# A hybrid decoder layer in float32 pairs: the order of cast, dependent work and low part in each step, both heads' scores in one step, banks emptied a step later, the norm two cycles later, and another order of the first output block

## The chip, the cores and the metric

The kernel runs on one core of a Trainium2 chip. The metric is the device time of one execution in microseconds (us), taken as the median of the runs. TensorE (PE in the profile; PEld is its weight load) multiplies matrices into eight PSUM banks. VectorE (DVE), ScalarE (ACT) and GpSimd (POOL) do the elementwise work, SyncE (SP) issues most of the transfers. Each engine works through its own instructions in order; semaphores hold an instruction back until what it reads or overwrites is ready.

## The reference

One layer of 16 stick-breaking attention heads beside 16 groups of a short gated convolution, for 256 tokens and 16 meta tokens, with 4096 channels:

```
h = rmsnorm(x, norm_g)
q, k, v, g_attn, b_conv, c_conv, h_conv, z_conv = split(h @ w_in)      # 4096 x 16384
z    = q . k / sqrt(128)                                # per head, strictly causal
a    = exp(log_sigmoid(z) + sum over later keys of log_sigmoid(-z))
o    = group_rmsnorm((a @ v) * silu(g_attn))
y    = group_rmsnorm(b_conv * conv3(c_conv * h_conv) * silu(z_conv))
out  = rmsnorm(x + concat(o, y) @ w_out)                # meta tokens dropped
```

## The kernel before

**Float32 from pairs.** Every weight tile arrives as `raw` (128 x 1024 float32). ACT casts it to `wh` (the high part, L399), DVE takes the rest `wl = raw - wh` (the **low part**, L395), and each product is three matmuls: low activations by `wh`, high activations by `wh`, high activations by `wl` (L424 to L426 for 258 columns, L432 to L435 for 512). `wh` and `wl` have rings of six buffers, so a tile is split five pieces ahead of its use.

**Pieces.** The program is a list of pieces, and the main loop (L970) goes through them one **step** a piece. The input projection has 8 groups of two heads. A piece `p` is a quarter of a projection block (k, v, c or h of one head, 24 matmuls). `A` and `B` are the two halves of a column pair of q, g, b, z for both heads (12 matmuls each). For the pairs listed in `SJ` (and `OUT_SJ` in the output projection) seven products do the work of eight: such a pair has four pieces A, B, T, U with 6, 3, 6 and 6 matmuls, T and U being sums of A and B that DVE forms (L409 to L414). I call such a pair a **seven**, the other a **plain** pair. Each group first has a **row zone** (R) of four plain pairs, with the last two blocks of the group before it between them (the order p p A B, four times), and then a **sum zone** (S) of twelve cycles A B T U p p. The output projection takes column blocks 8 to 11 of 16 pairs each, and eight narrow pieces at the end. A piece `m` reloads and casts a mixed activation tile that an earlier group has written to DRAM, and holds no matmul.

**What a step issues, before:** the matmuls of piece i; the split of piece i+5 (cast, and low part or the sums right behind it); the emptying of PSUM banks of what ended with piece i (`plain_block`, `open_rows`, `evict`, `out_sums`, `out_block`); then the tasks that are due (`run_tasks`). From the end of group 0 up to the eighth piece from the end the engines' order is the order in which the program issues (`manual_schedule`, L982).

**Tasks of a group** (`plan_group`, L828), counted in steps from `f`, the last step of the group's sum zone: the gates' SiLU and the transposition of q at f+1; for the two heads `scores` at f+4 and f+6, `weights` at f+7 and f+9, `trans` at f+10 and f+13, `po` at f+13 and f+17. `scores` is two matmuls `z`, one step later the mask on DVE (`zm`, L744, L746) and Abs, Tanh and Ln on ACT (L749 to L751). `weights` is one subtraction, two running sums and another subtraction on DVE (L757 to L761), one step later four Exp on ACT (`za`, L768 to L771). `trans` is a transposition on DVE (`ya`, L777) and, over the next two steps, copies of 32 x 96 squares into the one buffer `at`, half on ACT (L565), half on DVE (L563). `po` multiplies `at` by v (L788 to L792). The v blocks go through a like transposition (`vt`, `yv`, `vv`; L577 to L591).

**In the sum zone of the next group** the earlier group's convolution is transposed (`ct`), its squares are summed, `norm` (11 small DVE instructions, L692 to L694) gives the factors, and `mix` transposes the result on PE into a bank (`mxh` for the attention half, `mxc` for the convolution half, L707). In this zone there is one bank for all of it, the one in which the p blocks are summed, so `mix` has to wait until the last p block there has been emptied (L572, L578, L597 or L602 on DVE).

Of the kernel before, what the change touches and what calls it, by code (L numbers as in the profile page):

```python
# [8 lines left out]
F32 = mybir.dt.float32  # L9
# [6 lines left out]
P = 128  # L16
# [30 lines left out]
OUT_FIRST = (0, 1, 2, 3, 4, 5, 6, 7, 8, 9, 10, 14, 11, 12, 13, 15)  # L47
OUT_SJ = (8, 9, 10, 11, 12, 13)

# [6 lines left out]
def sevens(g):  # L56

    return OUT_SJ if g >= GROUPS else SJ if g else ()

# [5 lines left out]
def in_pieces():  # L65
# [45 lines left out]
def kernel(ctx, tc, xt, xin, xm, par, fg, w1, w2, out):  # L111
# [7 lines left out]
    wk.tile([P, 16], F32, name="pad_wk")  # L119
# [30 lines left out]
    ms = [("m", g) for g in range(GROUPS - 1)]  # L150
# [207 lines left out]
    def split(i):  # L358
# [9 lines left out]
        if p[0] == "m":  # L368
# [3 lines left out]
            nc.vector.tensor_tensor(out=lo, in0=t, in1=h.bitcast(F32), op=ALU.subtract)  # L372
# [8 lines left out]
            return  # L381
# [15 lines left out]
        for q in range(parts):  # L397
            c = slice(q * w // parts, (q + 1) * w // parts)
            nc.scalar.copy(out=h[:, c], in_=t[:, c])  # L399
            if not two or p[0] == "A":  # L400
                low(c)
        if two and p[0] == "A":
            sums[p] = t
        elif two:

            a = sums.pop(("A",) + p[1:])
            s = wp.tile([P, 1024], F32, tag="tt", name=f"t{i}", bufs=1)
# [7 lines left out]
            sums[("T",) + p[1:]], sums[("U",) + p[1:]] = s, t  # L415
# [199 lines left out]
    def plain_block(u, b, e):  # L615
# [3 lines left out]
        elif b == 1:  # L619
            v_block(u, ps[:, :L], after(e, 6 if u % 2 == 0 else 3))  # L620
# [114 lines left out]
    def scores(g, u):  # L735
        q = gr[g]["h"][0]
        kt = hd[2 * g + u, "k"]
        z = bank(f"z{g}_{u}")
        T.matmul(out=z[:, :144], lhsT=q[:, 0, u], rhs=kt[:, :144], start=True, stop=True)
        T.matmul(out=z[:, 144:ZW], lhsT=q[:, 1, u], rhs=kt, start=True, stop=True)  # L740
        yield 1
        zm = wk.tile([P, 512], F32, tag="u2", name=f"zm{g}_{u}", bufs=2) if u else wk.tile([P, 448], F32, tag="zm", name=f"zm{g}_{u}")
        zm = zm[:, :ZW]
        V.scalar_tensor_tensor(out=zm[:, :144], in0=z[:, :144], scalar=rq[:, 0:1], in1=zmask[:, P:],  # L744
                               op0=ALU.mult, op1=ALU.add)
        V.scalar_tensor_tensor(out=zm[:, 144:], in0=z[:, 144:ZW], scalar=rq[:, 1:2], in1=zmask,  # L746
# [365 lines left out]
```

## Time and profile before

| what | value |
|---|---|
| median of 3 runs | 1938.75 us (1937.78 to 1939.67) |
| the profiled execution | 1940.01 us, of which the span of the trace is 1938.1 us |
| PE, DVE, ACT, POOL busy | 95%, 81%, 59%, 7% of the span |
| mean granted clock of TensorE | 0.972 |
| from group to group (start of step f+1) | 195.5 us first, then 194.6 to 195.1 us |
| transfers | 393.64 MB, 203 GB/s in the mean |

The span is the time from the first to the last instruction; the rest of the execution lies around it. A busy PE is not a PE at its peak, since matmuls overlap. So the table is read as "PE is the engine on which nearly everything waits", and the question is where it stands idle or at a low clock.

### The profile page before, as it was taken

Reading aid. Unit: us, or ns where it says so; the run is one execution under the profiler, and the core shown is the slowest. Engines: PE = TensorE matmul, PEld = TensorE weight load, DVE = VectorE, ACT = ScalarE, POOL = GpSimd, SP = SyncE. Lnnn points to the kernel's source line nnn. Section 1 sums busy time; section 2 is a strip of 40 time slices with the busy share of each in tenths; the row PEclk is TensorE's granted clock in tenths of the full one; section 3 lists DMA queues with packets and bytes.
Section 4 is the critical chain, followed back from the end, with each engine's and each line's share of the span. In section 5 each row is a group of like instructions: output and inputs, shape, how many; then the busy total and the mean of one; then the engine's idle time right before and its main releaser. Section 6 shows DMA issues by size and latency. Waiting matters only on the chain.

```text
span 1938.1 us, 29646 instructions
## 1 busy us (share of the span) xinstructions
PE 1844.5 (95%) x10998; PEld 1653.0 (85%) x10998; DVE 1563.0 (81%) x2114; ACT 1147.1 (59%) x1756; POOL 136.6 (7%) x192
## 2 busy tenths in 40 slices
PE   9999899989998999899989998999899989999997
PEld 7899798979897989798979897989798967788897
DVE  6766788778877887788778887888788878998986
ACT  6645655655566556656565656565656575555554
POOL 2021010001000100010001000100010122000000
PEclk9999899989998999999999999999999989999999
DMA  8965456645664566456635663566366655575665
GB/s 306 317 222 191 153 200 222 207 151 197 218 217 143 199 222 220 142 196 220 226 140 197 218 227 136 201 211 235 134 205 207 229 173 182 193 246 205 230 204 185
DMA packets 116064, 393.64 MB, mean 203 GB/s; under 512 B 13008, under 2 KB 18256, under 8 KB 115920
## 3 DMA queue, kind: packets, MB, share of 16 engines
q1 hardware_dynamic: 111888, 388.08, 58.4%
q10 hardware_dynamic: 4032, 3.67, 0.5%
q8 instruction: 86, 1.41, 0.3%
q14 instruction: 58, 0.48, 0.1%
HBM read 380.17 MB, written 11.53 MB: 202 GB/s over the span
## 4 chain that ended last, share of the span: by engine, by line
PE 81%; DVE 8%; ACT 7%; issue 3%; DMA 1%; POOL 0%; DVEq 0%; ACTq 0%; SPq 0%; POOLq 0%
PE P L432 14%; PE P L434 14%; PE P L435 14%; PE mm L424 11%; PE mm L425 11%; PE mm L426 11%; DVE wl L395 3%; ACT wh L399 2%; DVE zl L759 1%; DVE at L563 1%; ACT L751 1%; ACT zl L751 1%; ACT L768 1%; ACT L750 1%; PE po L792 0%
## 5 line engine op out<-in xcount | busy, mean ns | idle before, releaser
L395 DVE TENSOR_TENSOR wl<-raw,wh 128x1024 fp32r<-128x1024 f32 (+3 forms) x756 | 852.3, 1145 | 267.9 <-ACT wh L399 256.6
L399 ACT CAST wh<-raw 128x1024 fp32r<-128x1024 f32 (+3 forms) x756 | 715.2, 974 | 396.3 <-PE mm L425 169.8
L424 PE MATMUL mm<-xs,wh 128*128 128x258 f32 (+1 forms) x2048 | 592.2, 289 | 0.0
L426 PE MATMUL mm<-xs,wl 128*128 128x258 f32 (+1 forms) x2048 | 588.7, 287 | 0.0
L425 PE MATMUL mm<-xs,wh 128*128 128x258 f32 (+1 forms) x2048 | 588.6, 287 | 0.0
L424 PEld LDWEIGHTS mm<-xs,wh 128*128 128x128 f32 x2048 | 390.8, 191 | 6.2 <-issue 1.6
L425 PEld LDWEIGHTS mm<-xs,wh 128*128 128x128 f32 x2048 | 390.7, 191 | 4.7
L426 PEld LDWEIGHTS mm<-xs,wl 128*128 128x128 f32 x2048 | 390.2, 191 | 0.0
L432 PE MATMUL P<-wh,xs 128*128 128x512 f32 x604 | 241.8, 400 | 2.1 <-ACT wh L399 2.1
L434 PE MATMUL P<-wh,xs 128*128 128x512 f32 x604 | 239.8, 397 | 0.0
L435 PE MATMUL P<-wl,xs 128*128 128x512 f32 x604 | 239.3, 396 | 0.0
L399 ACT CAST wh<-t 128x1024 fp32r<-128x1024 f32 (+1 forms) x108 | 112.3, 1040 | 169.4 <-DVE t L409 145.6
L432 PE MATMUL P<-wh,mixl 128*128 128x512 f32 (+1 forms) x392 | 149.9, 382 | 4.4 <-ACT wh L399 4.1
L435 PE MATMUL P<-wl,mixh 128*128 128x512 f32 (+1 forms) x392 | 149.6, 382 | 1.3 <-DVE wl L395 1.2
L434 PE MATMUL P<-wh,mixh 128*128 128x512 f32 (+1 forms) x392 | 148.9, 380 | 0.0
L435 PEld LDWEIGHTS P<-wl,xs 128*128 128x128 f32 x604 | 114.0, 189 | 27.6
L432 PEld LDWEIGHTS P<-wh,xs 128*128 128x128 f32 x604 | 114.4, 189 | 26.0 <-ACT wh L399 2.3
L434 PEld LDWEIGHTS P<-wh,xs 128*128 128x128 f32 x604 | 114.1, 189 | 22.5
L409 DVE TENSOR_TENSOR t<-raw,raw 128x1024 f32<-128x1024 f32 (+1 forms) x108 | 132.2, 1224 | 0.4
L395 DVE TENSOR_TENSOR wl<-t,wh 128x1024 fp32r<-128x1024 f32 (+1 forms) x108 | 131.9, 1221 | 0.0
L432 PEld LDWEIGHTS P<-wh,mixl 128*128 128x128 f32 x392 | 74.7, 190 | 17.5 <-ACT wh L399 4.5
L435 PEld LDWEIGHTS P<-wl,mixh 128*128 128x128 f32 x392 | 74.4, 190 | 15.5 <-DVE wl L395 3.5
(249 smaller groups left out, 2084.7 us busy)
## 6 DMA issues: line engine op xcount, KB each, us to landing
raw<-w SPq DMA_DIRECT2D x614, 512.0 KB, 4.2
lent<-sumd SPq DMA_DIRECT2D x49, 512.0 KB, 5.9
raw<-w SPq DMA_DIRECT2D x32, 384.0 KB, 4.0
raw<-xin SPq DMA_DIRECT2D x8, 512.0 KB, 5.0
xr<-xt SPq DMA_DIRECT2D x15, 272.0 KB, 5.4
sumd<-lent SPq DMA_DIRECT2D x7, 512.0 KB, 2.9
raw<-mixd SPq DMA_DIRECT2D x7, 512.0 KB, 4.3
res<-xin SPq DMA_DIRECT2D x12, 256.0 KB, 4.6
```

Of the source, the lines that this page charges most:

```text
L395: nc.vector.tensor_tensor(out=lo[:, c], in0=t[:, c], in1=h[:, c].bitcast(F32), op=ALU.subtract)
L399: nc.scalar.copy(out=h[:, c], in_=t[:, c])
L409: nc.vector.tensor_tensor(out=s[:, :2 * hw].rearrange("p (a b) -> p a b", a=2), in0=a[:, :2 * hw].rearrange("p (a b) -> p a b", a=2), in1= ...
L424: nc.tensor.matmul(out=o, lhsT=h, rhs=x[:, 0, s:], start=k == 0, stop=False)
L425: nc.tensor.matmul(out=o, lhsT=h, rhs=x[:, 1, s:], start=False, stop=False)
L426: nc.tensor.matmul(out=o, lhsT=lo, rhs=x[:, 0, s:], start=False, stop=k == KC - 1)
L432: nc.tensor.matmul(out=o, lhsT=a[1], rhs=h, start=key not in begun, stop=False)
L434: nc.tensor.matmul(out=o, lhsT=a[0], rhs=h, start=False, stop=False)
L435: nc.tensor.matmul(out=o, lhsT=a[0], rhs=lo, start=False, stop=last)
L563: V.tensor_copy(out=o, in_=x)
L750: A.activation(out=l, in_=l, func=AF.Tanh, scale=0.5)
L751: A.activation(out=l, in_=l, func=AF.Ln, scale=0.5, bias=half)
```

## The change

Six things are changed; the arithmetic of each is as it was, but for two pairs of the first output block.

1. Within a step the program now issues the cast, then the tasks, then the low part or the sums (`split` returns a closure, `lows` runs it at the step's end). Up to the end of group 0's first zone the low part still follows its cast.
2. `plain_block`, `open_rows`, `evict`, `out_sums` and `out_block` become tasks of the next step.
3. `scores` takes both heads: four matmuls at f+3, both masks, Abs and Tanh at f+4, both Ln at f+5.
4. `weights` moves to f+6 and f+8, `trans` to f+8 and f+10, `po` to f+11 and f+14. The SiLU of the second half goes to f+2, the transposition of v to the step in which its block is emptied.
5. In the sum zone `squares` goes from slot 4 to 5, `norm` from behind slot 4 to slot 6, `mix` from slots 6 and 8 to 8 and 10 (slot c is piece B of the cycle c, counted from 0).
6. The first output block takes its pairs in another order, pairs 12 and 13 are plain there, and the pieces `m` stand at other places.

```diff
-OUT_FIRST = (0, 1, 2, 3, 4, 5, 6, 7, 8, 9, 10, 14, 11, 12, 13, 15)
+OUT_FIRST = (0, 1, 2, 3, 4, 5, 6, 8, 7, 9, 14, 10, 15, 11, 12, 13)
+MIXED = {(1, "A"): 2, (3, "A"): 3, (5, "A"): 4, (6, "B"): 5, (9, "A"): 6}
-    return OUT_SJ if g >= GROUPS else SJ if g else ()
+    return OUT_SJ[:4] if g == GROUPS else OUT_SJ if g > GROUPS else SJ if g else ()
...
-            v_block(u, ps[:, :L], after(e, 6 if u % 2 == 0 else 3))
+            v_block(u, ps[:, :L], after(e, 1))
...
-    def scores(g, u):
+    def scores(g):
         q = gr[g]["h"][0]
+        z, zm, l = {}, {}, {}
+        for u in range(2):
+            kt = hd[2 * g + u, "k"]
+            z[u] = bank(f"z{g}_{u}")
+            T.matmul(out=z[u][:, :144], lhsT=q[:, 0, u], rhs=kt[:, :144], start=True, stop=True)
+            T.matmul(out=z[u][:, 144:ZW], lhsT=q[:, 1, u], rhs=kt, start=True, stop=True)
         yield 1
...
+            A.activation(out=l[u], in_=zm[u], func=AF.Abs)
+        for u in range(2):
+            A.activation(out=l[u], in_=l[u], func=AF.Tanh, scale=0.5)
+        yield 1
+        for u in range(2):
+            A.activation(out=l[u], in_=l[u], func=AF.Ln, scale=0.5, bias=half)
+            gr[g]["z", u] = zm[u], l[u]
...
         later(after(f, 1), silu, g, "h")
-        later(after(f, 1), silu, g, "c")
         later(after(f, 1), q_t, g)
-        for u, at_ in enumerate(((4, 7, 10, 13), (6, 9, 13, 17))):
-            for k, fn in zip(at_, (scores, weights, trans, po)):
+        later(after(f, 2), silu, g, "c")
+        later(after(f, 3), scores, g)
+        for u, at_ in enumerate(((6, 8, 11), (8, 10, 14))):
+            for k, fn in zip(at_, (weights, trans, po)):
                 later(after(f, k), fn, g, u)
...
+        later(slot(g + 1, 5), squares, g, "c")
+        later(slot(g + 1, 6), norm, g)
+        later(slot(g + 1, 8), mix, g, "h")
+        later(slot(g + 1, 10), mix, g, "c")
...
+        while halved < until:
+            lows()
+            r = split(halved)
+            halved += 1
+            if r:
+                rest.append(r)
+        if i <= top[0]:
+            lows()
...
-                plain_block(*p[1], i)
+                later(i + 1, plain_block, *p[1], i)
...
-                evict(p[1])
+                later(i + 1, evict, p[1])
...
         run_tasks(i)
+        lows()
```

**ACT in the row zone**, heads of group 4: what stands from the second head's Abs to the first head's Exp. `zl4_0` and `zl4_1` are the two heads' logarithms, `za` their weights, `wh428` the cast of piece 428. Before:

```order
L399 CAST wh428_9821<-raw428_9692 128x1024
L749 ACTIVATE zl4_1_9833<-zm4_1_9830 128x416
L750 ACT_TABLE_LOAD
L750 ACTIVATE zl4_1_9833<-zl4_1_9833 128x416
L751 ACT_TABLE_LOAD
L751 ACTIVATE zl4_1_9833<-zl4_1_9833,half_120 128x416
L399 CAST wh429_9851<-raw429_9722 128x1024
L768 ACT_TABLE_LOAD
L768 ACTIVATE za4_0_9855<-zs4_0_9825 128x256
```

Now, from the first head's Abs on:

```order
L762 ACTIVATE zl4_0_9738<-zm4_0_9737 128x416
L762 ACTIVATE zl4_1_9743<-zm4_1_9742 128x416
L764 ACTIVATE zl4_0_9738<-zl4_0_9738 128x416
L764 ACTIVATE zl4_1_9743<-zl4_1_9743 128x416
L401 CAST wh426_9776<-raw426_9634 128x1024
L767 ACT_TABLE_LOAD
L767 ACTIVATE zl4_0_9738<-zl4_0_9738,half_120 128x416
L767 ACTIVATE zl4_1_9743<-zl4_1_9743,half_120 128x416
L401 CAST wh427_9808<-raw427_9679 128x1024
L401 CAST wh428_9831<-raw428_9720 128x1024
L784 ACT_TABLE_LOAD
L784 ACTIVATE za4_0_9836<-zs4_0_9811 128x256
```

The first head's Exp no longer stands behind the second head's Abs, Tanh and Ln, and two table loads are gone: a group now has three of them, where it had five.

**DVE at the same place.** `zs` and the scans into `zl` are the weights, `wl429` is the low part of piece 429. Before:

```order
L757 SCALAR_TENSOR_TENSOR zs4_0_9825<-zm4_0_9752,zl4_0_9755 128x416
L759 SCALAR_TENSOR_TENSOR zl4_0_9755<-one_118,zs4_0_9825 128x144
L759 SCALAR_TENSOR_TENSOR zl4_0_9755<-one_118,zs4_0_9825 128x272
L761 TENSOR_TENSOR zs4_0_9825<-zm4_0_9752,zl4_0_9755 128x416
L744 SCALAR_TENSOR_TENSOR zm4_1_9830<-z4_1_9804,rq_124,zmask_113 128x144
L746 SCALAR_TENSOR_TENSOR zm4_1_9830<-z4_1_9804,rq_124,zmask_113 128x272
L395 TENSOR_TENSOR wl429_9852<-raw429_9722,wh429_9851 128x1024
L395 TENSOR_TENSOR wl430_9891<-raw430_9772,wh430_9890 128x1024
L757 SCALAR_TENSOR_TENSOR zs4_1_9894<-zm4_1_9830,zl4_1_9833 128x416
```

Now:

```order
L777 TENSOR_TENSOR zs4_0_9811<-zm4_0_9737,zl4_0_9738 128x416
L397 TENSOR_TENSOR wl427_9809<-raw427_9679,wh427_9808 128x1024
L607 TENSOR_TENSOR cc9_9834<-mm9_2_9590,rstd_122 128x258
L397 TENSOR_TENSOR wl428_9832<-raw428_9720,wh428_9831 128x1024
L793 STREAM_TRANSPOSE ya4_0_9860<-za4_0_9836 128x448
L773 SCALAR_TENSOR_TENSOR zs4_1_9862<-zm4_1_9742,zl4_1_9743 128x416
```

The second head's mask has left this place (it stands with the first one's, a few steps earlier), and the low parts stand behind the step's dependent work.

**DVE in the sum zone**, the cycle of slot 6 of group 5 (pieces 469 to 474). `vv10` are copies of the transposed v block, `cc10` empties the p block out of the shared bank, which `mxh` takes before the change at piece 470. Before:

```order
L395 TENSOR_TENSOR wl469_10743<-raw469_10653,wh469_10742 128x1024
L563 COPY vv10_10730<-yv10_10718 32x2x32 x4
L409 TENSOR_TENSOR t470_10770<-raw469_10653,raw470_10688 128x1024
L412 TENSOR_TENSOR raw470_10688<-raw469_10653,t470_10770 128x512
L395 TENSOR_TENSOR wl470_10768<-raw470_10688,wh470_10767 128x512
L414 TENSOR_TENSOR raw470_10688<-raw470_10688 128x512
L395 TENSOR_TENSOR wl471_10784<-t470_10770,wh471_10783 128x1024
L395 TENSOR_TENSOR wl472_10814<-raw470_10688,wh472_10813 128x1024
L395 TENSOR_TENSOR wl473_10844<-raw473_10759,wh473_10843 128x1024
L597 TENSOR_TENSOR cc10_10847<-mm10_2_10655,rstd_122 128x258
```

Now:

```order
L397 TENSOR_TENSOR wl471_10762<-t470_10748,wh471_10761 128x1024
L397 TENSOR_TENSOR wl472_10792<-raw470_10685,wh472_10791 128x1024
L397 TENSOR_TENSOR wl473_10822<-raw473_10737,wh473_10821 128x1024
L607 TENSOR_TENSOR cc10_10834<-mm10_2_10656,rstd_122 128x258
L397 TENSOR_TENSOR wl474_10832<-raw474_10753,wh474_10831 128x1024
L702 TENSOR_SCALAR ss4_10126<-ss4_10126 128x8
```

The emptying stands at the same place among the low parts as before; the v copies have moved ahead by five pieces, and the norm (it begins with L702) now stands behind it. `mxh` now comes at piece 482, `mxc` at 494.

More of the change, by code (lines that the diff above doesn't have):

```diff
@@ L100, in in_pieces @@
         block(*t)
-        out += [("m", k) for k in ((), (0,), (1,), (2, 3))[i]]
+        if i in (1, 3):
+            out.append(("m", i // 2))
     zone += [("Z", GROUPS - 1)] * (len(out) - len(zone))
@@ L149 @@
     ends, fin, top = {}, {}, {}
-    ms = [("m", g) for g in range(GROUPS - 1)]
     for i, p in enumerate(pieces):
@@ L399, in split @@
             nc.scalar.copy(out=h[:, c], in_=t[:, c])
-            if not two or p[0] == "A":
+            if parts == 2:
                 low(c)
+        if parts == 2:
+            return
         if two and p[0] == "A":
@@ L404, in split, with rest @@
         elif two:
+            s = wp.tile([P, 1024], F32, tag="tt", name=f"t{i}", bufs=1)
+            sums[("T",) + p[1:]], sums[("U",) + p[1:]] = s, t
+        def rest():
+            if not two or p[0] == "A":
+                low(slice(0, w))
+                return
             a = sums.pop(("A",) + p[1:])
-            s = wp.tile([P, 1024], F32, tag="tt", name=f"t{i}", bufs=1)
             c1, c2 = slice(0, hw), slice(hw, 2 * hw)
@@ L976 @@
         until = min(i + SPLITS + ahead + 1, n)
-        while i < 0 and halved < until:
-            split(halved)
-            halved += 1
-        if i < 0:
-            continue
         if i == top[0] + 1:
@@ L986 @@
             fixed.close()
-        p, now[0] = pieces[i], i
-        if "all" not in hd:
-            free[0] = spare(i)
+        now[0] = i
+        p = pieces[max(i, 0)]
+        if i >= 0:
+            if "all" not in hd:
+                free[0] = spare(i)
+            if i < n1 or p[0] in "ABTUm":
+                mm_in(i)
+        while halved < until:
[6 more added lines that the diff above has]
+            lows()
+        if i < 0:
+            continue
         if i < n1:
-            mm_in(i)
-            while halved < until:
-                split(halved)
-                halved += 1
             if p[0] == "p" and p[2] == 3:
-                plain_block(*p[1], i)
+                later(i + 1, plain_block, *p[1], i)
             if i in plain_end.values():
-                open_rows(p[1])
+                later(i + 1, open_rows, p[1])
             if i in top.values():
-                evict(p[1])
+                later(i + 1, evict, p[1])
                 if p[1] == GROUPS - 1:
@@ L1005 @@
         elif p[0] in "ABTUm":
-            mm_in(i)
             g = p[1]
-            if p[0] == "U" and p[2] == OUT_SJ[-1]:
-                out_sums(g)
-            while halved < until:
-                split(halved)
-                halved += 1
+            if p[0] == "U" and p[2] == sevens(g)[-1]:
+                later(i + 1, out_sums, g)
             if p[0] == "B" and p[2] in (10, 6):
```

74 lines of the change are left out of this document (37 added, 37 removed).

## The prediction

> **What bounds the kernel now.** I read the page first, then PE's waits, then stretches of the program between the starts of chosen pieces.
>
> ```profile
> span 1938.1 us, 29646 instructions
> PE 1844.5 (95%) x10998; PEld 1653.0 (85%) x10998; DVE 1563.0 (81%) x2114; ACT 1147.1 (59%) x1756; POOL 136.6 (7%) x192
> ...
> PE 81%; DVE 8%; ACT 7%; issue 3%; DMA 1%; POOL 0%; DVEq 0%; ACTq 0%; SPq 0%; POOLq 0%
> ```
>
> PE is the engine on which the end hangs: the rest of the chain that ended last, DVE and ACT, is the time for which PE stood. PE's own waits (us in total, times, longest) say where:
>
> ```profile
> PE po L788 <- DVE at L563: 41.2, 7, 5.9
> PE mxh L707 <- DVE cc L597: 21.7, 7, 3.1
> ```
>
> Both come once at each of the seven passages from one group to the next: the first head's `po` waits for the copies into `at`, and `mxh` waits until the p block is emptied from the shared bank. What each costs I read from windows (length, then busy times, the granted clock, the DMA share) and from like stretches without the wait. First `po`: step f+13 to the start of f+16, pieces p p A.
>
> ```profile
> 791.57:810.44 18.87, 12.98 (x71) 11.82 (x70) 16.04 (x32) 9.85 (x27) 0.00 (x0) 0.82 0.32 111
> sum 133.31, PE 92.13 PEld 83.94 DVE 112.27 ACT 69.01 POOL 0.00; mean PE 13.16 PEld 11.99 DVE 16.04 ACT 9.86 POOL 0.00
> ...
> 780.22:791.57 11.35, 11.35 (x73) 10.27 (x72) 4.08 (x7) 9.18 (x13) 0.96 (x3) 1.00 0.41 149
> 810.44:822.81 12.37, 12.37 (x70) 10.67 (x69) 12.04 (x21) 8.13 (x16) 0.00 (x0) 1.00 0.58 207
> 822.81:833.70 10.89, 10.89 (x71) 9.96 (x70) 8.45 (x10) 5.72 (x7) 0.00 (x0) 1.00 0.55 197
> ...
> 1677.10:1682.54 5.44, 5.44 (x26) 4.51 (x25) 5.30 (x9) 2.17 (x6) 0.00 (x0) 1.00 0.64 227
> ```
>
> The first row is one such stretch, the sum is over all seven. Pieces p p A B without a wait take 11.35 us, and B is half a plain pair, 2.8 (2.7 by the last row, of the output stage, where a plain pair takes 5.44); so p p A is 8.55. `po` itself is what a cycle with it has more than one without: 12.37 - 10.89 = 1.48. Without the wait a stretch would take 10.03 us and seven 70.2: **63.1 us** are lost at `po`, 9.0 each, of which 5.9 are idle and 3.1 a low clock (0.82 in the stretch). Now the sum zone's cycle with `mxh` beside the one with `mxc`, one row each and the sums over seven:
>
> ```profile
> 879.93:895.75 15.82, 12.73 (x75) 11.21 (x74) 14.09 (x15) 8.95 (x11) 0.00 (x0) 0.89 0.72 249
> sum 110.89, PE 89.21 PEld 78.35 DVE 98.64 ACT 62.60 POOL 0.00; mean PE 12.74 PEld 11.19 DVE 14.09 ACT 8.94 POOL 0.00
> ...
> 906.36:917.69 11.33, 11.33 (x76) 10.35 (x74) 10.35 (x14) 6.52 (x8) 0.00 (x0) 1.00 0.72 246
> sum 79.24, PE 79.24 PEld 72.43 DVE 72.35 ACT 45.66 POOL 0.00; mean PE 11.32 PEld 10.35 DVE 10.34 ACT 6.52 POOL 0.00
> ```
>
> `mxc` does the same work and does not wait: 110.89 - 79.24 = **31.65 us** are lost at `mxh`. In these rows an idle of 3.1 us lowers the clock as well (0.89). The Trainium skill ("TensorE: Matmul & The Clock Gate", Part 1) drops the clock to half after an idle window of about 3.4 us; by that alone this term would be the idle time only, 21.7, but the rows have more, and I go by them.
>
> **The change at `po`.** These rows (ACT, then DVE) are the fourth passage before the change; in brackets stands the idle time ahead.
>
> ```profile
> 782.30 0.55 ACT L749 ACTIVATE zl<-zm 128x416 f32<-128x416 f32 x1 [4.73 <-DVE zm L746]
> 784.74 1.28 ACT L751 ACT_TABLE_LOAD   x1
> 786.03 0.65 ACT L751 ACTIVATE zl<-zl,half 128x416 f32<-128x416 f32 x1
> 787.63 1.28 ACT L768 ACT_TABLE_LOAD   x1
> 789.66 1.99 ACT L399 CAST wh<-raw 128x1024 fp32r<-128x1024 f32 x2
> ...
> 779.27 0.58 DVE L757 SCALAR_TENSOR_TENSOR zs<-zm,zl 128x416 f32<-128x416 f32 x1
> 781.50 0.36 DVE L744 SCALAR_TENSOR_TENSOR zm<-z,rq,zmask 128x144 f32<-128x144 f32 x1
> 781.78 0.49 DVE L746 SCALAR_TENSOR_TENSOR zm<-z,rq,zmask 128x272 f32<-128x272 f32 x1
> 787.65 1.23 DVE L395 TENSOR_TENSOR wl<-raw,wh 128x1024 fp32r<-128x1024 f32 x1 [5.38 <-ACT wh L399]
> 795.25 0.64 DVE L777 STREAM_TRANSPOSE ya<-za 128x448 f32<-128x448 f32 x1
> 799.44 0.91 DVE L563 COPY at<-ya 32x96 f32<-32x96 f32 x4
> 800.38 0.17 DVE L783 COPY at<-ya 16x16 f32<-16x16 f32 x1
> ```
>
> ACT stands 4.73 us for DVE's mask, and DVE then 5.38 us for a cast that is queued on ACT behind the second head's Abs, Tanh, Ln and two table loads. The two engines wait for each other in turn, and the first head's Exp, a task of f+8, comes after 788. The change cuts both waits: the mask stands with the first head's, and dependent work stands ahead of the low part that waits for the cast. Is the new chain short enough for `po` at f+11? I lay the rows end to end from the moment both `z` are there (end of f+3):
>
> - DVE may be late here by 1.0 (below); both masks 2 x 0.77; then Abs of the second head and two Tanh, 0.55 each: 4.2.
> - ACT: cast 1.0, table 1.28, two Ln 1.3: 7.8, the first at 7.2.
> - DVE: the first head's weights 2.23 (779.27 to 781.50) to 9.4, a low part, an emptying of 0.42, a low part: 12.3. ACT meanwhile: two casts, table and four Exp 2.03 (787.63 to 789.66): 11.8.
> - DVE: transposition 0.64, weights of the second head 2.23, low 1.23, copies 0.91, low 1.23, transposition 0.64, copies 0.91 and two small ones 0.3: 20.4.
>
> PE by then has B, p p A B, p p A, that is two times 11.35 = 22.7 us. The chain is in time by 2.3 us. The second head has the same copies behind the first `po` and 8.5 us until its own: in time by more than 4. So the wait goes, and behind it I find nothing that is late next: the `at` copies of the second head stand in ACT's and DVE's queues for some 2 to 3 us behind PE's first `po`, with casts and low parts behind them, but those are for pieces five ahead, some 8 us or more. Term: -63.1. If the cover fails, each us of lateness past 2.3 costs a us seven times, and a low clock from about 3 on.
>
> The late start of 1.0 comes from POOL, whose clearing of `vt`'s end now stands behind the first two SiLU products (it stood ahead of them):
>
> ```profile
> 758.73 2.03 POOL L665 TENSOR_TENSOR cq<-cq,sgh 128x256 f32<-128x256 f32 x2 [79.53 <-PE mm L426]
> 760.73 2.44 POOL L665 TENSOR_TENSOR cb<-cb,sgc 128x256 f32<-128x256 f32 x2
> ...
> 760.83 1.73 DVE L395 TENSOR_TENSOR wl<-raw,wh 128x1024 fp32r<-128x1024 f32 x1 [1.35 <-ACT wh L399]
> ```
>
> Cast, table, a sigmoid of about 0.5 and 2.03 make 4.8; DVE's v transposition waits for that, and it, two sets of copies and three low parts follow (6.2): 11.0, where `z` is there at 10.4. Those rows also show DVE slower beside POOL, 1.73 for 1.23. The Trainium skill ("SBUF — State Buffer", Who interferes with whom) says why: POOL and DVE instructions with two SBUF inputs lock one port pair, and the loser stands still. By that rule the second SiLU half, now a step later, can take its whole 2.44 us from DVE just ahead of the masks; the trace agrees in kind (0.5 us). That is a rival below.
>
> **The change at `mix`.** Before, the emptying comes 4.8 us after its block ended at 879.9; the v copies and the norm lie ahead of it. A cycle later, at the place to which `mxh` now goes, it is in time:
>
> ```profile
> 884.72 0.42 DVE L597 TENSOR_TENSOR cc<-mm,rstd 128x258 f32<-128x258 f32 x1
> 906.56 0.43 DVE L602 TENSOR_TENSOR cc<-mm,cc 128x258 f32<-128x258 f32 x1 [0.39 <-PE mm L426]
> ...
> 908.45 0.60 PE L707 MATMUL mxc<-ident,cb 128*128 128x128 f32 x4
> ...
> 865.53 0.16 DVE L692 TENSOR_SCALAR ss<-ss 128x8 f32<-128x8 f32 x1
> 867.55 0.17 DVE L694 TENSOR_TENSOR ss<-n,fac 128x8 f32<-128x8 f32 x1
> ...
> 895.75:906.36 10.61, 10.61 (x71) 9.69 (x70) 9.07 (x9) 5.69 (x6) 0.00 (x0) 1.00 0.46 159
> ```
>
> Here DVE waits for PE (0.39), and PE's transposition has 1.46 us to spare (906.99 to 908.45). The norm (11 instructions, 2.2 us from its first to its last) now comes 11 pieces ahead of that emptying, nearly two cycles with 1.54 us free in each (10.61 - 9.07). That pays for the norm; its eight multiplications on ACT hold casts up as well, for which I count up to 0.8 of lateness. It fits into 1.46. `mxc`, one cycle on, has more room. Each us of lateness past 1.46 would cost a us seven times. Term: -31.65, between 0 and that.
>
> **The last stage** of the order, steps 681 to the end of output block 8:
>
> ```profile
> 1534.08:1671.01 136.93, 121.53 (x605) 99.88 (x603) 112.00 (x154) 85.23 (x146) 30.04 (x36) 0.95 0.54 183
> 1693.56:1698.42 4.86, 4.86 (x22) 3.94 (x21) 4.83 (x5) 3.37 (x4) 0.00 (x0) 1.00 0.59 181
> ```
>
> Without waits it would be eight p (5.75 a pair, 11.35 less 5.6) 23.0, ten plain pairs 54.4, six sevens of 4.86 29.2, and some 6 for `po` and transpositions: 112.6. So 24.3 are lost. The change makes two sevens plain (+1.2) and takes from DVE their sums and extra low parts, some 4.4 each, so its 112 become 103; sevens now alternate with plain pairs. It also shortens the head's chain as above. But this stage has reloaded tiles (a cast and a low part each, no matmul), so DVE's chain is late by 1 to 3 at the first `po`, and where the sevens begin its low parts come just in time. I count 5.8 of waits left: 1.2 + 112.6 + 5.8 = 119.6, a term of -17.3, between +1.2 (all waits stay) and -23.1 (none).
>
> **What is added.** The emptying of the sum zone's banks starts behind one cast more (1.0), and the next p block and q's transposition need two of these banks: between 0 and 7, I take +2.5. The output blocks' banks are emptied a step later too; there two plain pairs, 10.9 us, lie ahead of their next use and cover it, so I cost that at nothing (uncovered, 1.0 a block). SP's transfers keep their order but for the reloads, which are issued eight pieces ahead.
>
> **Sum:** 63.1 + 31.65 + 17.3 - 2.5 = 109.6 off 1940.0, the profiled execution (1.9 of it around the span), gives 1830.4; the median before was 1.3 less, so **1829 us**.
>
> **The rivals.**
> - *The bank stays late* (0.12): the emptying at piece 481 is as late as at 468 before, since DVE has 119 us of work in a sum zone of 131 or so. For it: its 14.09 of 15.82. Against: 0.39 of waiting for PE a cycle later. The 31.65 stay: 1861.
> - *The `at` chain stays partly late* (0.10): POOL takes its 4.5 us from DVE instead of some 0.6; 2.3 of that is covered, seven times 1.6 to 6: 1840 to 1875.
> - *DVE takes PE's place* (0.03): what PE no longer waits at two places it waits all over. Against it DVE's 81%. No change: 1938.
> - *Slower* (0.03): one buffer `at`. ACT and DVE stand at the second head's copies until PE's first `po`, now in the same step; before, a step lay between. I count 2 to 3 us. It costs nothing up to the 8 us of work that PE has split ahead, and makes the kernel slower from 8 plus the gain of 109.6 / 7 = 15.7, about 24 us: then 1945 or more.
> - That the change doesn't move what it says is ruled out by the engines' order.
>
> **How the numbers follow.** The forecast has 0.72: 1816 (all of the last stage, nothing added) to 1848. The first two rivals reach to 1875; taking 1861 in leaves out half of the second, the third and the fourth. Range 1815 to 1862. A measurement here can tell about 0.2% (4 us) from no change: faster 0.94, same 0.02, slower 0.04.
>
> **What would show it.** PE's waits without `po` on `at` and with `mxh` or `mxc` under 1 us each; a mean clock near 0.99; a passage from group to group of 181 us; three table loads a group; the last stage at 115 to 125 us. I am wrong if DVE's idle time for casts in the row zone stays at 5 us, or if PE's waits reappear at the first p block of a row zone.

## The result and the profile after

The changed kernel takes **1808.4 us** (median of 4 runs, 1806.1 to 1808.5) where the kernel before, run beside it, takes 1938.9 (1937.8 to 1939.7): a ratio of 0.932, 95% interval 0.931 to 0.934. The forecast was 1829, from 1815 to 1862; the gain is 130.6 us where 109.6 were forecast. So some 21 us came from something the prediction did not have.

The page of the changed kernel, the lines that answer to those shown of before:

```profile
span 1806.7 us, 29670 instructions
PE 1784.4 (99%) x11004; PEld 1618.5 (90%) x11004; DVE 1555.5 (86%) x2104; ACT 1120.3 (62%) x1736; POOL 144.5 (8%) x192
...
PE 93%; DVE 3%; ACT 1%; POOL 1%; DMA 1%; issue 1%; SPq 0%; DVEq 0%; POOLq 0%; ACTq 0%
```

PE is busy for 99% of the span and makes 93% of the chain that ended last (95% and 81% before). PE's own waits, longest first (us in total, times, longest):

```profile
PE P L442 <- ACT wh L401: 4.0, 2, 2.5
PE mo L933 <- DVE res L908: 2.8, 1, 2.8
PE qT L741 <- DVE vt L588: 1.7, 3, 1.2
```

`po` and `mxh` are gone from the list. The only long wait that is new stands at the end of the program (`mo`). Now windows over the seven passages, from the start of f+1 to the end of the sum zone's first cycle, so that both heads' `po` lie inside in both kernels (length, busy times, granted clock, DMA share). The fourth passage and the sum of all, before:

```profile
755.71:825.61 69.90, 64.01 (x392) 57.73 (x390) 49.13 (x83) 44.45 (x83) 5.40 (x7) 0.95 0.45 157
sum 490.54, PE 449.36 PEld 405.34 DVE 342.32 ACT 311.15 POOL 36.46; mean PE 64.19 PEld 57.91 DVE 48.90 ACT 44.45 POOL 5.21
```

And after:

```profile
702.09:762.40 60.31, 60.31 (x391) 54.99 (x390) 50.21 (x84) 41.58 (x81) 5.53 (x8) 1.00 0.54 176
sum 423.18, PE 422.65 PEld 384.98 DVE 348.83 ACT 290.90 POOL 38.34; mean PE 60.38 PEld 55.00 DVE 49.83 ACT 41.56 POOL 5.48
```

The length is now PE's busy time, at a clock of 1.00. But the sums differ by 67.4 us, 4.3 more than the 63.1 that the wait was worth. The same in a cycle of the sum zone in which nothing waited before, and in which the change moves nothing. The sum over its seven occurrences, before:

```profile
sum 76.21, PE 76.21 PEld 69.70 DVE 63.48 ACT 40.32 POOL 0.00; mean PE 10.89 PEld 9.96 DVE 9.07 ACT 5.76 POOL 0.00
```

After:

```profile
sum 74.76, PE 74.76 PEld 69.03 DVE 63.46 ACT 39.78 POOL 0.00; mean PE 10.68 PEld 9.86 DVE 9.07 ACT 5.68 POOL 0.00
```

PE is busy without a gap in both, with the same matmuls, and needs 10.68 us in place of 10.89. So the missing 21 us seem to lie not in a wait, but in the matmuls themselves.

### The profile page after: what moved, and what is told of

It is laid out like the page before. It is cut to its first block, busy times and chain, and to the rows that moved or that the text cites. A ratio compares the mean times of both kernels' runs of the same rounds, so it can differ in the third digit from the quotient of the medians.

```text
span 1806.7 us, 29670 instructions
## 1 busy us (share of the span) xinstructions
PE 1784.4 (99%) x11004; PEld 1618.5 (90%) x11004; DVE 1555.5 (86%) x2104; ACT 1120.3 (62%) x1736; POOL 144.5 (8%) x192
## 4 chain that ended last, share of the span: by engine, by line
PE 93%; DVE 3%; ACT 1%; POOL 1%; DMA 1%; issue 1%; SPq 0%; DVEq 0%; POOLq 0%; ACTq 0%
PE P L442 16%; PE P L445 16%; PE P L444 16%; PE mm L436 13%; PE mm L435 13%; PE mm L434 13%; DVE wl L397 1%; DMA raw<-w 1%; ACT wh L401 1%; PE mo L933 0%; PE mo L935 0%; PE mo L934 0%; POOL sfo L308 0%; PE z L752 0%; PE po L808 0%
## 5 line engine op out<-in xcount | busy, mean ns | idle before, releaser
L397 DVE TENSOR_TENSOR wl<-raw,wh 128x1024 fp32r<-128x1024 f32 (+2 forms) x754 | 849.3, 1147 | 121.6 <-ACT wh L401 110.8
L401 ACT CAST wh<-raw 128x1024 fp32r<-128x1024 f32 (+2 forms) x754 | 714.1, 976 | 379.6 <-PE mm L435 109.4
L434 PE MATMUL mm<-xs,wh 128*128 128x258 f32 (+1 forms) x2048 | 582.7, 285 | 0.0
L435 PE MATMUL mm<-xs,wh 128*128 128x258 f32 (+1 forms) x2048 | 581.8, 284 | 0.0
L436 PE MATMUL mm<-xs,wl 128*128 128x258 f32 (+1 forms) x2048 | 581.6, 284 | 0.0
L435 PEld LDWEIGHTS mm<-xs,wh 128*128 128x128 f32 x2048 | 385.6, 188 | 4.1
L434 PEld LDWEIGHTS mm<-xs,wh 128*128 128x128 f32 x2048 | 385.5, 188 | 4.1
L436 PEld LDWEIGHTS mm<-xs,wl 128*128 128x128 f32 x2048 | 385.6, 188 | 0.0
L442 PE MATMUL P<-wh,xs 128*128 128x512 f32 x604 | 238.6, 395 | 1.5 <-ACT wh L401 1.5
L445 PE MATMUL P<-wl,xs 128*128 128x512 f32 x604 | 235.5, 390 | 0.2
L444 PE MATMUL P<-wh,xs 128*128 128x512 f32 x604 | 235.4, 390 | 0.0
```

Of the source, the lines that this page charges most:

```text
L397: nc.vector.tensor_tensor(out=lo[:, c], in0=t[:, c], in1=h[:, c].bitcast(F32), op=ALU.subtract)
L434: nc.tensor.matmul(out=o, lhsT=h, rhs=x[:, 0, s:], start=k == 0, stop=False)
L435: nc.tensor.matmul(out=o, lhsT=h, rhs=x[:, 1, s:], start=False, stop=False)
L436: nc.tensor.matmul(out=o, lhsT=lo, rhs=x[:, 0, s:], start=False, stop=k == KC - 1)
L442: nc.tensor.matmul(out=o, lhsT=a[1], rhs=h, start=key not in begun, stop=False)
L444: nc.tensor.matmul(out=o, lhsT=a[0], rhs=h, start=False, stop=False)
```

## Experiments: the missing 21 us

The diff has one line that the prediction gives no term and that the cut diff above leaves out: an unused tile, `pad_wk`, becomes 32 words wide instead of 16. Every tile behind it in SBUF moves by 64 bytes: `raw`, `wh`, `wl`, the sums and the mixed activation tiles `mixh` and `mixl` go from 64 bytes past a multiple of 128 to a multiple. `xs` is allocated from the other end and stays.

**That line alone, in the kernel before.**

```diff
-    wk.tile([P, 16], F32, name="pad_wk")
+    wk.tile([P, 32], F32, name="pad_wk")
```

> The kernel before with nothing changed but the unused tile pad_wk, 32 words wide instead of 16: every tile of the pools that lie behind it (raw, wh, wl, the sums) starts 64 bytes later. Theory 'address': the 512-wide matmuls take 227 ns from start to start instead of 233 and the 258- and 272-wide ones 121.5 instead of 124.3, since wh and wl now start at a multiple of 128 bytes; the cycles of the sum zone that wait for nothing lose 0.1 to 0.2 us each (10.89 to 10.68), and the kernel 15 to 25 us: 1914 to 1924. Rival 'order': the faster matmuls of the changed kernel come from its order, and this edit is worth nothing: 1939, within 3.

Measured: 1920.9 us, ratio 0.991 (0.990 to 0.993), 18.5 us below the runs of before beside it (1939.4). **That line undone, in the changed kernel.**

> The changed kernel with pad_wk 16 words wide, as it was before; all else as changed. Theory 'address': matmuls back at 233 ns, 15 to 25 us slower, 1823 to 1834, where the forecast had it (1829). Rival 'order': 1808, within 3.

Measured: 1828.2 us, ratio to before 0.943 (0.941 to 0.945): 19.8 us are the line's, and the rest of the change gives 111.2 (1939.4 - 1828.2), where 109.6 were forecast. A window of twelve 512-wide matmuls in the row zone, in the kernel before:

```profile
777.42:780.22 2.80, 2.80 (x14) 2.26 (x12) 2.77 (x5) 0.16 (x1) 0.00 (x0) 1.00 0.45 152
```

The same in that kernel with the wider pad:

```profile
767.50:770.22 2.72, 2.72 (x14) 2.25 (x12) 2.69 (x5) 0.16 (x1) 0.00 (x0) 1.00 0.45 116
```

And in the changed kernel with the old pad:

```profile
734.58:737.38 2.80, 2.80 (x14) 2.26 (x13) 2.62 (x5) 1.45 (x6) 0.00 (x0) 1.00 0.93 366
```

2.80 / 12 is 233 ns a matmul, 2.72 / 12 is 227, at a granted clock of 1.00 in all three: the pad makes it, whatever the order. The casts and low parts do not care. Their groups before (mean ns of one behind the comma):

```profile
L395 DVE TENSOR_TENSOR wl<-raw,wh 128x1024 fp32r<-128x1024 f32 x612 | 742.9, 1233 | 260.7 <-ACT wh L399 250.2
L399 ACT CAST wh<-raw 128x1024 fp32r<-128x1024 f32 x612 | 628.6, 1048 | 367.6 <-PE mm L425 169.8 <-DVE raw L414 79.1 <-PE P L434 59.1
```

And after:

```profile
L397 DVE TENSOR_TENSOR wl<-raw,wh 128x1024 fp32r<-128x1024 f32 x612 | 741.2, 1235 | 116.1 <-ACT wh L401 106.3
L401 ACT CAST wh<-raw 128x1024 fp32r<-128x1024 f32 x612 | 628.8, 1050 | 355.0 <-PE mm L435 109.4 <-DVE raw L423 80.5 <-issue 74.0
```

**Which tile's place counts.** In the kernel before, 64 bytes ahead of `wh` (so `raw` and the small tiles stay), and `xs` moved alone:

```diff
+            if i == 0:
+                wp.tile([P, 16], F32, name="pad_h", bufs=1)
             h = wp.tile([P, 1024], F32R, tag="wh", name=f"wh{i}", bufs=RING)
```

> The kernel before with an unused tile of 64 bytes between raw and wh: wh, wl and the sums move by 64 bytes, raw and all smaller tiles stay. If the start of the operands that PE reads (or that ACT and DVE write) counts: as with the wider pad, 1914 to 1924. If it is raw (the target of the loads) or a small tile whose place counts: 1939, within 3.

```diff
-    xp.tile([P, 40], F32, name="pad_x")
+    xp.tile([P, 24], F32, name="pad_x")
```

> The kernel before with xs moved by 64 bytes to a multiple of 128 and wh, wl left at 64 past one. If the place of wh and wl alone counts: 1939, within 3. If it is the place of xs and wh to one another, or xs's own: 15 to 25 us faster, or slower by a few us.

Measured: 1918.7 us (0.989, 0.988 to 0.991) and 1938.9 us (1.000, 0.999 to 1.001). The place of `raw` is worth nothing, nor is that of `xs` as long as `wh` and `wl` lie off the multiple (with these on it, it was not tried); the places of `wh`, `wl` and what lies behind them are. Then in the changed kernel, `wh` and `wl` apart, and both at another offset:

```diff
             h = wp.tile([P, 1024], F32R, tag="wh", name=f"wh{i}", bufs=RING)
+            if i == 0:
+                wp.tile([P, 16], F32, name="pad_l", bufs=1)
             lo = wp.tile([P, 1024], F32R, tag="wl", name=f"wl{i}", bufs=RING)
```

> The changed kernel with pad_wk at 16 words and 64 unused bytes between wh and wl: wh at 64 past a multiple of 128, wl (and the sums) at a multiple. If the start of the tile that a matmul streams counts by itself: the two matmuls of a product with wh take 233 ns each, the one with wl 227, and the kernel loses some 60% of the 20 us: 1818 to 1822. If it is the write of the cast into wh, or all of the three slow down together: 1826 to 1830.

> The changed kernel with wh at a multiple of 128 bytes and wl (and the sums) 64 past one, the mirror of the run with wh at 64 and wl at a multiple, which took 1839.1. If a difference between the two tiles is what slows all three matmuls of a product: 1835 to 1843 again. If it is wh's own place: 1808 to 1814. If each tile's place costs its own share: 1813 to 1818.

(this second one with `pad_wk` at 32 and `pad_w` at 24 words), and `pad_wk` at 24 words:

> The changed kernel with pad_wk 24 words wide: raw, wh, wl and the sums all start 96 bytes past a multiple of 128 (at a multiple in the changed kernel, 64 past one before). If any start off a multiple of 128 costs the same: 1826 to 1830. If a start off a multiple of 64 costs more: 1835 and up. If only 64 is bad: 1808.

Bytes past a multiple of 128, the us of the cycle shown above, and the time of the kernel:

| `wh` | `wl` | cycle | kernel, us | ratio to before (95%) |
|---|---|---|---|---|
| 0 | 0 | 10.68 | 1808.4 | 0.932 (0.931 to 0.934) |
| 64 | 64 | 10.89 | 1828.2 | 0.943 (0.941 to 0.945) |
| 96 | 96 | 10.94 | 1827.9 | 0.942 (0.941 to 0.944) |
| 0 | 64 | 10.89 | 1830.4 | 0.944 (0.942 to 0.946) |
| 64 | 0 | 10.98 | 1839.1 | 0.949 (0.948 to 0.950) |

That any start off a multiple costs the same held for the two tiles together. For the tiles apart none of the theories held: the cost is not shared between the two, and it does not go by their difference alone. One tile off the multiple costs as much as both, and `wh` off with `wl` on costs more. The sums, `mixh` and `mixl` lay with `wl` in both of these runs. How PE's reads come to that is open. Last, the changed kernel with `raw` and the small tiles put back where they were and `wh`, `wl` at a multiple:

> The changed kernel with pad_wk at 16 words and 64 unused bytes ahead of wh: wh, wl and the sums at multiples of 128 as in the changed kernel, raw and the small tiles where they were before. If only what PE reads counts: 1808, within 3. In the kernel before, this edit gave 20.8 us where the wider pad gave 18.5; if that is real, the changed kernel gains some 2 too: 1805 to 1807.

Measured: 1806.9 us (0.932, 0.931 to 0.934), no difference that can be told.

## Experiments: the rest of the change

**The two cuts at `po`, one by one and together.** First the order:

```diff
             if r:
-                rest.append(r)
+                r()
```

> The changed kernel with each low part directly behind its cast again, ahead of the step's dependent work; the joint scores and all times stay. Theory 'both cuts are needed' (the forecast's: DVE stood 5.4 us at a low part whose cast was queued behind the head's work): the first po waits again, 3 to 9 us at each of seven passages, and the kernel takes 1830 to 1870. Rival 'the joint scores alone': the chain is in time without the order, 1808 to 1812.

Measured: 1840.3 us (0.950, 0.948 to 0.951). Then the scores apart, with the function of before and the squares behind the later `po`:

```diff
-        later(after(f, 3), scores, g)
-        for u, at_ in enumerate(((6, 8, 11), (8, 10, 14))):
-            for k, fn in zip(at_, (weights, trans, po)):
+        for u, at_ in enumerate(((4, 7, 10, 13), (6, 9, 13, 17))):
+            for k, fn in zip(at_, (scores, weights, trans, po)):
```

> The changed kernel with each head's scores apart again, at the steps that they had before (f+4 and f+6, po at f+13 and f+17; the squares behind them as before); the low part stays behind the dependent work. Theory 'both cuts are needed': with five table loads a group and the second head's mask late, the first po waits again, 2 to 9 us a passage: 1822 to 1870. Rival 'the order alone': 1808 to 1812.

Measured: 1820.9 us (0.939, 0.937 to 0.941). And both:

> The changed kernel with both cuts at po undone: the scores of each head apart at their old steps, and each low part directly behind its cast. Undone one by one they cost 12.5 and 31.9 us, and in neither did the first po wait as before. Theory 'either cut is enough': with both undone the wait of some 6 us and the low clock come back, 9 us a passage on top of the sum: 1853 + 40 to 65 = 1890 to 1920. Rival 'something else took the wait away' (the emptying a step later, v's transposition earlier): the two costs just add, 1848 to 1858, and po does not wait.

Measured: 1899.5 us (0.980, 0.979 to 0.981). DVE's wait for casts, and PE's for `at`, in the waits of the kernel with both undone:

```profile
DVE wl L397 <- ACT wh L401: 260.3, 196, 5.4
...
PE po L798 <- DVE at L573: 28.5, 7, 4.1
```

The same two and those at the mixes with the order alone undone:

```profile
DVE wl L397 <- ACT wh L401: 204.9, 196, 2.5
...
PE po L804 <- DVE at L573: 5.5, 8, 2.9
...
PE mxc L717 <- DVE kT L582: 5.1, 7, 0.7
...
PE mxh L717 <- DVE cc L612: 4.9, 7, 0.7
```

And DVE's in the changed kernel:

```profile
DVE wl L397 <- ACT wh L401: 110.8, 131, 1.7
```

The sums over the seven passages (423.2 in the changed kernel), first with the order undone:

```profile
sum 428.67, PE 424.80 PEld 384.83 DVE 341.40 ACT 289.89 POOL 40.45; mean PE 60.69 PEld 54.98 DVE 48.77 ACT 41.41 POOL 5.78
```

With the scores apart:

```profile
sum 425.58, PE 424.78 PEld 384.72 DVE 345.79 ACT 310.57 POOL 34.07; mean PE 60.68 PEld 54.96 DVE 49.40 ACT 44.37 POOL 4.87
```

With both undone:

```profile
sum 478.37, PE 448.36 PEld 405.29 DVE 340.90 ACT 309.15 POOL 36.10; mean PE 64.05 PEld 57.90 DVE 48.70 ACT 44.16 POOL 5.16
```

5.5, 2.4 and 55.2 us: **either cut removes the wait nearly whole, and only without both does it come back.** My theory that both are needed fell. In the fourth passage DVE's two longest stands for a cast are 4.10 and 5.37 us with both undone, 2.50 and 2.21 with the order undone, and 2.96 and 4.23 with the scores apart, where the head's work stands ahead of the low parts. Each cut alone is only just enough: there `po` still waits 0.37 us with the order undone, and `at` is there 0.4 us ahead of it with the scores apart. What the order is worth beyond `po` are 0.6 to 0.7 us at each of `ct`, `mxh` and `mxc` in every group (14.5 us in all), whose inputs or banks DVE otherwise gets to behind a low part. With the passages, the last stage (124.7 us for 121.3) and the stretch behind the last `P` matmul (40.6 for 38.7) that makes some 25 of its 31.9 us; the rest stays open. What the joint scores are worth beyond `po` lies in the last stage: 130.4 us from piece to piece with the scores apart, 121.3 in the changed kernel.

**The norm and the mixes at their old cycles.**

```diff
-        later(slot(g + 1, 5), squares, g, "c")
-        later(slot(g + 1, 6), norm, g)
-        later(slot(g + 1, 8), mix, g, "h")
-        later(slot(g + 1, 10), mix, g, "c")
+        later(slot(g + 1, 4), squares, g, "c")
+        later(after(slot(g + 1, 4), 1), norm, g)
+        later(slot(g + 1, 6), mix, g, "h")
+        later(slot(g + 1, 8), mix, g, "c")
```

> The changed kernel with squares, norm and mixes back at cycles 4, 6 and 8 of the sum zone. Theory of the forecast: the last p block's bank is emptied too late for mxh, by 4.5 us and more, since the emptying now starts a step later: 32 to 55 us slower, 1840 to 1863. Rival: the low parts that stand behind the emptying now made it early enough: 1808 to 1815.

Measured: 1820.8 us (0.939, 0.937 to 0.941), 12.4 slower and between the two. PE waits again, in its waits

```profile
PE mxh L717 <- DVE cc L607: 11.5, 7, 1.7
```

but for less than before the change (3.1 us and a low clock), and at full clock, by the window of that cycle in the last group (the clock is the third number from the end):

```profile
1365.62:1378.45 12.83, 11.19 (x75) 9.98 (x74) 12.54 (x13) 8.36 (x10) 0.00 (x0) 1.00 0.76 263
```

So the later cycle makes only 12.4 of what `mxh` lost; the rest went although the emptying is issued a step later. DVE's rows ahead of the emptying `cc` tell where. In the kernel before (the emptying itself is the row at 884.72 in the prediction):

```profile
872.12 1.23 DVE L395 TENSOR_TENSOR wl<-raw,wh 128x1024 fp32r<-128x1024 f32 x1 [0.89 <-ACT wh L399]
...
874.87 0.78 DVE L563 COPY vv<-yv 32x64 f32<-32x64 f32 x4
...
877.15 0.79 DVE L563 COPY vv<-yv 32x64 f32<-32x64 f32 x4
```

And with the old cycles:

```profile
816.78 3.50 DVE L397 TENSOR_TENSOR wl<-raw,wh 128x1024 fp32r<-128x1024 f32 x3 [0.90 <-ACT wh L401]
...
826.94 0.42 DVE L607 TENSOR_TENSOR cc<-mm,rstd 128x258 f32<-128x258 f32 x1
```

From the low part that waited for its cast to the emptying are 12.60 us before and 10.16 here, with the same low parts and sums between; what is missing are v's transposition and two sets of its copies (2.04 us), which the change moved five pieces ahead, and one wait of 0.24. The emptying now comes 3.3 us behind the end of its block at 823.64, where it came 4.8 behind. By these rows the moved v copies are the other part; undoing them alone was not tried.

**The first output block as before.**

```diff
-OUT_FIRST = (0, 1, 2, 3, 4, 5, 6, 8, 7, 9, 14, 10, 15, 11, 12, 13)
+OUT_FIRST = (0, 1, 2, 3, 4, 5, 6, 7, 8, 9, 10, 14, 11, 12, 13, 15)
...
-    return OUT_SJ[:4] if g == GROUPS else OUT_SJ if g > GROUPS else SJ if g else ()
+    return OUT_SJ if g >= GROUPS else SJ if g else ()
```

> The changed kernel with the first output block's column pairs in the order of before and six of them in seven products; the reloads stay where the change put them. The forecast put 1.2 us on the added products and took some 9 us of DVE's work away: by that the block loses its spare time again and the kernel is 4 to 16 us slower, 1812 to 1824. Rival: the block's waits went by the head's shorter chain alone, and six sevens save PE 1.2 us: 1805 to 1808.

Measured: 1815.6 us (0.936, 0.935 to 0.938), 7.3 slower. Of these the trace shows 2.4 in the stage itself (123.7 for 121.3) and 3.6 in the next output block (86.8 for 83.2), where PE now waits for low parts (8 times, up to 1.2 us).

**The banks emptied in the same step.**

```diff
-                later(i + 1, plain_block, *p[1], i)
+                plain_block(*p[1], i)
...
-                later(i + 1, open_rows, p[1])
+                open_rows(p[1])
...
-                later(i + 1, evict, p[1])
+                evict(p[1])
```

> The changed kernel with a bank emptied in the step of its last matmuls again (rows, sum zone and plain blocks; the output blocks stay as changed). The forecast costed the later emptying at 2.5 us, between 0 and 7: by that undoing it gives 1802 to 1808. Rival: a step later costs nothing, since the next p block comes later still, and the early emptying only stands in front of the step's cast and low part: 1808 to 1815.

The output blocks' banks stay a step later here. Measured: 1808.5 us (0.933, 0.932 to 0.934), no difference that can be told. **The new wait at the end.** I undid the later step for the last output block alone, first for its banks, then for its sums:

```diff
-                later(i + 1, out_blocks, g)
+                if g == GROUPS + 3:
+                    out_blocks(g)
+                else:
+                    later(i + 1, out_blocks, g)
```

> The changed kernel with the last output block's banks emptied in the step of its last matmuls; all other emptyings stay a step later. In the changed kernel PE stands 2.8 us for these banks (for res at L908) ahead of the first mo matmul, and the matmuls behind it take 0.21 us instead of 0.12 at a low clock; from the last P matmul to the end are 38.7 us, 34.9 before the change. Theory: the later emptying costs that, and without it the time is 3 to 5 us less, 1803 to 1806. Rival: casts and low parts of the last pieces stand ahead of the emptying anyway: 1808, within 2.

```diff
-                later(i + 1, out_sums, g)
+                if g == GROUPS + 3:
+                    out_sums(g)
+                else:
+                    later(i + 1, out_sums, g)
```

> The changed kernel with the last output block's four sums (out_sums, whose first addition at L908 is what PE's mo waits for) issued in the step of their last matmuls; all else a step later as changed. Theory: ACT's copy os then stands behind one cast instead of two, DVE's addition behind one low part less, PE's wait goes from some 3 us to under 1.5 and the low clock behind it goes: from the last P matmul to the end 35 to 36 us instead of 38.7, 1803 to 1806. Rival: one cast ahead is enough to keep it late: 1808, within 2.

Measured: 1805.7 us (0.931, 0.930 to 0.933) and 1803.5 us (0.930, 0.929 to 0.932). With the banks early PE's wait stays (3.4 us), and from the last `P` matmul to the end are 39.5 us, no less than the 38.7 of the changed kernel. What this run is faster by lies elsewhere, in the last stage (117.8 us for 121.3), which the edit does not touch. The sums shorten the wait. PE's timeline at the first `mo` matmuls (start, duration of one, in brackets the idle time ahead), changed kernel:

```profile
1770.76 0.58 PE L933 MATMUL mo<-keep,mixl 128*128 128x256 f32 x1 [2.79 <-DVE res L908]
1771.14 0.41 PE L934 MATMUL mo<-keep,mixh 128*128 128x256 f32 x1
1771.35 0.41 PE L935 MATMUL mo<-keep,mixh 128*128 128x256 f32 x1
```

The window of that stretch:

```profile
1770.70:1774.20 3.50, 3.44 (x17) 3.44 (x18) 3.50 (x9) 2.02 (x4) 0.00 (x0) 0.56 0.00 0
```

With the sums early, the timeline:

```profile
1767.68 0.39 PE L933 MATMUL mo<-keep,mixl 128*128 128x256 f32 x1 [2.08 <-DVE res L908]
1767.90 0.28 PE L934 MATMUL mo<-keep,mixh 128*128 128x256 f32 x1
1768.02 0.28 PE L935 MATMUL mo<-keep,mixh 128*128 128x256 f32 x1
```

And the window:

```profile
1767.60:1771.00 3.40, 3.32 (x27) 3.32 (x28) 3.40 (x9) 2.45 (x5) 0.00 (x0) 1.00 0.05 20
```

With 0.7 us less of idle time the clock behind it stays at 1.00. From the last `P` matmul to the end of the span are 36.7 us, 38.7 in the changed kernel, 34.9 before. These 2.0 us are the part of the 4.9 that the run shows; the rest lies in the last stage (118.1 for 121.3), which this edit does not touch and which took 117.8 to 121.3 in runs whose edits leave it alone. Both tail edits together, with `wh` and `wl` placed as in the run with `raw` put back:

> The changed kernel with what the runs so far point to: the last output block's sums and banks emptied in the step of their last matmuls, wh, wl and the sums at multiples of 128 bytes, raw and the small tiles where they were before the change. 1802 to 1806; not above 1808.

Measured: 1804.9 us (0.931, 0.930 to 0.932), not better than the sums alone: the lowest of all the runs is the changed kernel with the last block's sums early, 1803.5. With both edits PE stands hardly longer ahead of `mo` than with the sums alone, 2.17 us for 2.08, and yet the clock falls behind it:

```profile
1767.13 0.39 PE L935 MATMUL mo<-keep,mixl 128*128 128x256 f32 x1 [2.17 <-DVE res L910]
...
1768.70:1772.10 3.40, 3.40 (x19) 3.40 (x18) 3.40 (x6) 1.05 (x1) 0.00 (x0) 0.50 0.00 0
```

So it is not the length of the idle time alone that decides on the clock; the last section comes back to it.

## Why the prediction missed, and where it held

**The step that failed** is the list of edits itself: the prediction has terms for the edits of the order (`po`, `mix`, the last stage, what is added) and none for the wider unused tile, so its cost was put at nothing without a word. It was worth 19.8 us, 15% of the whole gain, and it alone puts the time below the range. With it undone, the changed kernel takes 1828.2 where 1829.0 were forecast. That this is within 1 us is in part luck: by the rows below, the gains came out 1.0 less, 1.95 more and 0.6 more than their terms, the losses 1.3 more. The steps can be checked against that run, whose tiles lie where they lay before. Its windows: the sums over the seven passages, over the sum zone's seventh cycle, in which `mxh` stood, and over the eleventh, in which `mxc` now stands (the ninth, which `mxc` left to `mxh`, keeps its length); and the last stage.

```profile
sum 428.42, PE 428.06 PEld 386.41 DVE 348.47 ACT 290.81 POOL 38.36; mean PE 61.15 PEld 55.20 DVE 49.78 ACT 41.54 POOL 5.48
...
sum 74.26, PE 74.26 PEld 67.83 DVE 65.37 ACT 53.29 POOL 0.00; mean PE 10.61 PEld 9.69 DVE 9.34 ACT 7.61 POOL 0.00
...
sum 79.30, PE 79.30 PEld 72.46 DVE 67.13 ACT 46.40 POOL 0.00; mean PE 11.33 PEld 10.35 DVE 9.59 ACT 6.63 POOL 0.00
...
1437.52:1556.59 119.07, 115.46 (x611) 97.70 (x609) 107.47 (x149) 80.34 (x141) 36.15 (x37) 1.00 0.64 215
```

The eleventh cycle in the kernel before:

```profile
sum 76.22, PE 76.22 PEld 69.72 DVE 66.58 ACT 40.03 POOL 0.00; mean PE 10.89 PEld 9.96 DVE 9.51 ACT 5.72 POOL 0.00
```

- **`po`:** 490.54 - 428.42 = 62.1 us, forecast 63.1. The size was right, and so was the chain. In the changed kernel `at` is there 2.5 us ahead of `po` (732.26 to 734.80; forecast 2.3), here ACT's and DVE's last copies and PE, in the timeline of the fourth passage:

```profile
730.37 1.15 ACT L575 COPY at<-ya 32x96 f32<-32x96 f32 x4
732.10 0.16 DVE L800 COPY a<-ya 16x16 f32<-16x16 f32 x1
734.80 0.38 PE L804 MATMUL po<-vv,at 128*128 128x128 f32 x2
```

  What the prediction did not see is that each of the two cuts would just about have done it alone. And other than the text on ACT's order ahead of the prediction says, the first head's Exp still stands behind the second head's Abs, Tanh and Ln; what is gone are two of a group's five table loads, and the wait for the second mask is down from 4.73 us to 0.19.
- **`mix`:** (110.89 - 74.26) - (79.30 - 76.22) = 33.6, forecast 31.65. The size was right; the reason only in part, since the later cycle by itself is worth 12.4. The rest comes, by DVE's rows above, from the v copies that no longer lie ahead of the emptying.
- **The last stage:** 136.93 - 119.07 = 17.9, forecast 17.3; 121.3 in the changed kernel, inside the 115 to 125 named as its sign.
- **What is added:** forecast 2.5 at the sum zone's banks; undoing the later emptying there gave nothing. The losses lie where I had costed the later step at nothing because two plain pairs lie ahead of the banks' next use: behind the last output block there is no further pair, PE stands 2.8 us for its sums and runs at 0.56 of its clock behind that. From the last `P` matmul to the end are 40.3 us in the run with the old pad, 5.4 more than before. The three gains above make 113.6 and the spans differ by 109.8, so 3.8 are lost in all; the term's size was near, its place wrong.
- **The signs:** no wait at `po`, `mxh` or `mxc`; clock 0.996; three table loads a group for five; DVE's longest wait for a cast 1.7 us for 5.4. A passage from group to group takes 181.1 us with the old pad, as forecast, and 178.5 in the changed kernel.
- **The rivals:** none came. The bank is in time, and with one buffer `at` ACT and DVE stand 2.65 and 2.37 us behind the first `po` (2 to 3 forecast), which costs nothing. POOL's price stayed small; these rows of the timeline after are POOL's second SiLU half and DVE beside it and after it:

```profile
706.87 0.74 POOL L675 TENSOR_TENSOR cb<-cb,sgc 128x256 f32<-128x256 f32 x1 [0.26 <-ACT sgc L674]
...
707.57 1.72 POOL L675 TENSOR_TENSOR cb<-cb,sgc 128x256 f32<-128x256 f32 x1
...
707.05 1.64 DVE L397 TENSOR_TENSOR wl<-raw,wh 128x1024 fp32r<-128x1024 f32 x1
...
709.97 1.23 DVE L397 TENSOR_TENSOR wl<-raw,wh 128x1024 fp32r<-128x1024 f32 x1
```

  The second half's 2.44 us, which the prediction took for one piece, are two multiplications (0.74 and 1.73 us before, 0.74 and 1.72 after). DVE's low part began inside the first and lost 0.41 us (1.64 for 1.23); the second multiplication began inside the low part and took 1.72 us for 0.74. Each lost about what was left of the other's instruction. The rule of the Trainium skill ("SBUF — State Buffer", Who interferes with whom) agrees with that; what DVE lost by it was the rest of one such instruction, not the whole 2.44.

## What to carry to other kernels

Give every line of a diff a term, an unused tile too: one that moves the tiles which matmuls read can be worth as much as a schedule, and it shows as a cycle without waits that changes its length. Where two edits go at one wait, undo them one by one and together before saying which did it. A timeline row with `x2` at its end is two instructions: split it before reading its time as the price of one. Where work is moved a step later under cover of what follows, look at the last time it happens: nothing follows there.

## What the runs showed of the hardware

- **Where PE's operands start.** With `wh` and `wl` at a multiple of 128 bytes a 512-wide matmul with `xs` as its stationary operand took 227 ns, 64 bytes past one 233, at the same granted clock and with casts and low parts as long as before; 18 to 21 us of each kernel. 96 bytes past cost the same, and one tile on the multiple and one off it 22 to 31 us. Not every matmul shows it: output blocks 9 and 10, whose stationary operands are mostly `mixh` and `mixl`, which move with `wl`, took 83.2 us with the multiple and 83.7 with both tiles off it, but 85.5 and 85.8 with one of them off.
- **The clock gate.** In all 19 traces the granted clock falls to 0.50 at marks 3.41 us apart that run through the whole execution, and then stays there for 3.41 us or a multiple, or to the end. Of the stretches between two such marks that had the full clock (without the first 100 and the last 27 us of each run), each of the 84 in which PE stood for more than 1.95 us was followed by the low clock, one of the 68 with 1.0 to 1.75 us was, and 6 of the 14 between. So an idle time of some 2 to 3.4 us can go either way: 2.17 us ahead of `mo` lowered the clock (1.85 of it between two marks), while 2.08 us there did not (0.82 and 1.25 on the two sides of a mark). And some 3.36 us at `mxh` in the kernel before with the wider pad lowered it at four of the seven passages and not at the other three: that the 3.1 us there in the kernel before lowered it every time does not follow from their length. The Trainium skill ("TensorE: Matmul & The Clock Gate", Part 1) puts the drop after an idle window of about 3.4 us. The length agrees; by these traces PE need stand for only a little over half of it.
